# 128 bytes of padding ahead of the raw and split weights of a three-pass float32 matmul kernel

## The chip, the cores and the metric

The kernel runs on one core of one Trainium2 chip, as one launch. The metric is the device time of a run in microseconds (us); lower is better. The engines are TensorE (PE; its weight loads are listed apart as PEld), VectorE (DVE), ScalarE (ACT), GpSimd (POOL) and SyncE (SP, which issues most of the transfers). [...]

## The reference, cut to what matters

A batch of one sequence, 512 tokens of 1024 channels, goes through three layers in float32:

- layer 0: a short convolution with gates beside a multi-head latent attention (8 heads), then a squared-ReLU MLP of width 4096;
- layer 1: a conformer convolution module (GLU, depthwise convolution of 31 taps, layer norm, SiLU), then the same kind of MLP;
- layer 2: a forgetting attention (8 heads, with 16 meta tokens put in front) beside trailing-mean pooling, then a SwiGLU feed-forward of width 2816.

```
proj = h @ w_in                        # 1024 x 2208
ffn  = square(relu(h @ w1)) @ w2       # 1024 x 4096, 4096 x 1024
ffn2 = (silu(n2 @ w_gate) * (n2 @ w_up)) @ w_down
```

Nearly all the work is in such products of an activation of 512 tokens with a weight matrix that is read once.

## The kernel before

**Three passes a product.** Every float32 operand is split in two `float32r` parts, a high part and the rest (low). `mm3` issues three matmuls for each block of 128 x 128 weights: high weights by high activation (line 357), high weights by low activation (line 358), low weights by high activation (line 359). The weight block is the *stationary* operand, which a weight load (LDWEIGHTS) brings into the array; the activation, 128 partitions by 512 tokens, is the *moving* operand that streams past it. The weight load of the next matmul runs while the current matmul streams.

**Tiles.** Activations live in tiles named `P` ("token tiles"), `[128, 2, 512]` of 4 bytes, so 4096 bytes a partition: the high half first, the low half 2048 bytes on. Scratch tiles `S` are `[128, 544]` floats, 2176 bytes. The weights arrive from memory in `raw` tiles of 4096 bytes (line 271, on SP's queue, three in rotation) and are split into `W` tiles, `[128, 2, 512]` as well: ScalarE writes the high half (line 284), VectorE the low half (line 286; GpSimd in one stretch). A `W` tile holds four blocks of 128 columns, 512 bytes apart. Some matmuls read no `W` tile at all: attention scores (line 623: keys stationary, queries moving), their maxima (line 872) and the values times probabilities (lines 357 to 359 through `mm3`) have a `P` tile on both sides.

**Where the tiles lie.** The pools stand behind one another in each partition, in the order of their `with` lines: constants, `p` (32 tiles of 4096 bytes), `s` (9 tiles of 2176), then `r` (`raw`, 3 of 4096) and `w` (`W`, 9 of 4096). The pools of PSUM and DRAM take no room there. 4096 is 16 times 256, so all `P` tiles begin at one offset within 256 bytes; 9 times 2176 is 19584, which is 76 times 256 and 128 over. So `raw` and `W` tiles begin 128 bytes off the `P` tiles within 256, and every 128-column block in them too, since blocks lie 512 bytes apart and halves 2048.

**Order.** The orders of the two attention parts are written out by hand (`B1`, `B2`); the rest follows loops. The weights come in exactly the order in which they are used, split four blocks ahead of TensorE.

```
mm(ps, w[0], x[0], start=first, stop=False)
mm(ps, w[0], x[1], start=False, stop=False)
mm(ps, w[1], x[0], start=False, stop=last)
```

Of the kernel before, what the change touches and what calls it, by code (L numbers as in the profile page):

```python
# [11 lines left out]
F32 = mybir.dt.float32  # L12
# [7 lines left out]
DRAM = bass.MemoryType.DRAM  # L20
# [1698 lines left out]
def build(arrays, stop=None):  # L1719
    nc = bacc.Bacc("TRN2", target_bir_lowering=False, num_devices=1)  # L1720
    ap = {}
    for name, a in arrays.items():
        ap[name] = nc.dram_tensor(f"in_{name}", a.shape, mybir.dt.from_np(a.dtype), kind="ExternalInput").ap()
    ap["out"] = nc.dram_tensor("out_0", (D, T), F32, kind="ExternalOutput").ap()
    with tile.TileContext(nc) as tc:
        with tc.tile_pool(name="c", bufs=1) as cp, tc.tile_pool(name="p", bufs=NP) as pp, \
                tc.tile_pool(name="s", bufs=NS) as sp, tc.tile_pool(name="ps", bufs=8, space=PSUM) as psp, \
                tc.tile_pool(name="d", bufs=1, space=DRAM) as dp, \
                tc.tile_pool(name="r", bufs=3) as rp, tc.tile_pool(name="w", bufs=NW) as wp:
            Program(tc, ap, (cp, pp, sp, psp, dp, rp, wp), stop).run()  # L1730
    return nc

# [6 lines left out]
```

## Time and profile before

| what | value |
|---|---|
| time, median of 3 runs | 1793.89 us (1792.48 to 1795.05) |
| the profiled execution: its own time, its span | 1788.58 us, 1786.8 us |
| TensorE busy with matmuls | 1746.1 us, 98% of the span, 8828 matmuls |
| VectorE, ScalarE, GpSimd busy | 1092.6 us, 802.0 us, 272.4 us |
| mean granted TensorE clock | 0.996 |
| transfers | 167.26 MB, mean 94 GB/s |

The profile is one execution, taken apart from the timed runs. The ends of matmuls in it are modelled and overlap (a matmul of 512 columns is listed with some 395 ns while the next one starts some 232 ns after it), so a matmul's cost is read from the starts: the distance from one start to the next, or a stretch without idle time divided by the matmuls that start in it.

### The profile page before, as it was taken

How to read it: one execution, taken by the hardware profiler on the slowest of the kernel's cores; microseconds unless marked ns; L12 is line 12 of the kernel's file. 1: busy time of each engine (PE TensorE's matmuls, PEld its weight loads, DVE VectorE, ACT ScalarE, POOL GpSimd, SP SyncE). 2: the span in 40 equal slices, each digit the busy share in tenths (PEclk: the TensorE clock that was granted, in tenths of full speed). 3: DMA queues.
4: the chain of work that ended last, by engine and by line, in shares of the span. 5: the costliest groups of instructions: out<-in, count | busy, mean ns of one | idle time of the engine just before them, and what ended most of it. 6: DMA issues, size and time to landing. Idle time of an engine off the chain costs nothing.

```text
span 1786.8 us, 23140 instructions
## 1 busy us (share of the span) xinstructions
PE 1746.1 (98%) x8828; PEld 1455.2 (81%) x8828; DVE 1092.6 (61%) x1770; ACT 802.0 (45%) x1461; POOL 272.4 (15%) x339
## 2 busy tenths in 40 slices
PE   9999999999999999999999999989999999999999
PEld 7778888888888878998888888888787888888887
DVE  7988685344444789968544444488896554344442
ACT  6546655333333446576433333357675443232230
POOL 3413330000000365503000000042223200000000
PEclk9999999999999999999999999999999999999999
DMA  5232213222222133512222222222222222222221
GB/s 200 68 101 59 101 60 118 94 95 94 95 94 95 48 106 106 166 59 91 100 95 94 95 95 95 94 95 73 72 73 95 94 95 94 95 94 95 94 95 59
DMA packets 49887, 167.26 MB, mean 94 GB/s; under 512 B 6848, under 2 KB 7296, under 8 KB 49776
## 3 DMA queue, kind: packets, MB, share of 16 engines
q1 hardware_dynamic: 47776, 160.70, 27.0%
q0 software_dynamic: 1936, 5.07, 1.0%
q8 instruction: 69, 1.13, 0.3%
q14 instruction: 42, 0.34, 0.1%
q10 hardware_dynamic: 64, 0.02, 0.0%
HBM read 158.25 MB, written 4.19 MB: 91 GB/s over the span
## 4 chain that ended last, share of the span: by engine, by line
PE 81%; DVE 11%; issue 3%; ACT 2%; POOL 2%; DMA 1%; SPq 0%; POOLq 0%; DVEq 0%; ACTq 0%
PE ps L358 26%; PE ps L357 26%; PE ps L359 26%; DVE P L968 2%; DVE W L286 1%; PE ps L623 1%; DVE P L401 1%; DVE S L424 1%; POOL P L971 1%; ACT S L450 1%; DVE S L1477 1%; DVE P L398 1%; DVE S L422 1%; DMA P<-in_xT 1%; DVE P L636 0%
## 5 line engine op out<-in xcount | busy, mean ns | idle before, releaser
L357 PE MATMUL ps<-P,W 128*128 128x512 f32 (+1 forms) x2541 | 935.2, 368 | 6.9 <-DVE S L1130 3.1
L358 PE MATMUL ps<-P,W 128*128 128x512 f32 (+1 forms) x2541 | 932.1, 367 | 5.8 <-DVE P L401 5.8
L359 PE MATMUL ps<-P,W 128*128 128x512 f32 (+1 forms) x2541 | 930.9, 367 | 0.0
L284 ACT ACTIVATE W<-raw 128x512 fp32r<-128x512 f32 x578 | 356.9, 628 | 672.9 <-PE ps L359 586.3
L286 DVE TENSOR_TENSOR W<-raw,W 128x512 fp32r<-128x512 f32 x523 | 372.2, 719 | 396.8 <-ACT W L284 391.1
L357 PEld LDWEIGHTS ps<-P,W 128*128 128x128 f32 x2541 | 479.9, 189 | 93.2 <-DVE S L1130 3.5
L358 PEld LDWEIGHTS ps<-P,W 128*128 128x128 f32 x2541 | 480.3, 189 | 90.2 <-DVE P L401 7.2
L359 PEld LDWEIGHTS ps<-P,W 128*128 128x128 f32 x2541 | 480.0, 189 | 84.4 <-DVE W L286 0.4
L971 POOL TENSOR_TENSOR P<-P 128x256 f32<-128x256 f32 x48 | 45.5, 957 | 787.9 <-DVE P L968 786.8
L398 DVE TENSOR_TENSOR P<-S,P 128x512 fp32r<-128x512 f32 (+3 forms) x134 | 93.8, 705 | 50.5 <-ACT P L397 49.9
L397 ACT ACTIVATE P<-S 128x512 fp32r<-128x512 f32 (+3 forms) x134 | 81.4, 613 | 63.2 <-DVE S L1664 25.8
L286 POOL TENSOR_TENSOR W<-raw,W 128x512 fp32r<-128x512 f32 x55 | 73.6, 1369 | 38.0 <-ACT W L284 33.9
L1082 DVE SCALAR_TENSOR_TENSOR ps<-P,vec,ps 128x512 f32<-128x512 f32 x116 | 77.8, 745 | 0.0
L1029 DVE SCALAR_TENSOR_TENSOR S<-ps,S 128x512 f32<-128x512 f32 x64 | 43.7, 690 | 37.0 <-PE ps L359 36.7
L400 ACT ACTIVATE P<-P,vec 128x256 fp32r<-128x256 f32 (+1 forms) x80 | 43.7, 550 | 49.8 <-POOL P L971 30.3
L470 POOL TENSOR_TENSOR S<-S 128x256 f32<-128x256 f32 (+1 forms) x45 | 47.6, 1058 | 76.0 <-ACT S L469 73.6
L401 DVE SCALAR_TENSOR_TENSOR P<-P,vec 128x256 fp32r<-128x256 f32 (+1 forms) x80 | 53.2, 678 | 9.7 <-ACT P L400 9.5
L469 ACT ACTIVATE S<-P 128x256 f32<-128x256 f32 (+1 forms) x105 | 46.4, 473 | 17.8 <-DVE P L1056 11.8
L636 POOL TENSOR_TENSOR P<-S,P 128x512 fp32r<-128x512 f32 (+1 forms) x24 | 34.3, 1428 | 113.0 <-DVE P L635 96.1
L1049 DVE TENSOR_TENSOR P<-ps,P 128x512 f32<-128x512 f32 x42 | 29.1, 692 | 30.9 <-PE ps L359 30.9
L623 PE MATMUL ps<-P 128*128 128x512 f32 (+3 forms) x160 | 41.3, 376 | 1.8 <-DVE S L1443 0.8
L470 DVE TENSOR_TENSOR S<-S 128x256 f32<-128x256 f32 (+1 forms) x60 | 33.0, 550 | 14.5 <-ACT S L469 13.5
(262 smaller groups left out, 1295.6 us busy)
## 6 DMA issues: line engine op xcount, KB each, us to landing
raw<-in_w SPq DMA_DIRECT2D x286, 512.0 KB
P<-in_xT SPq DMA_DIRECT2D x8, 256.0 KB
P<-in_xT POOLq DMA_DIRECT2D x8, 256.0 KB, 5.6
keep<-P SPq DMA_DIRECT2D x8, 256.0 KB
P<-P SPq DMA_DIRECT2D x16, 128.0 KB
P<-keep POOLq DMA_DIRECT2D x8, 256.0 KB, 4.6
out<-P SPq DMA_DIRECT2D x7, 256.0 KB
raw<-in_w SPq DMA_DIRECT2D x2, 256.0 KB
```

The source lines that it names most:

```text
L284: nc.scalar.activation(out=w[:, 0, :cols], in_=r, func=AF.Copy)
L286: eng.tensor_sub(out=w[:, 1, :cols], in0=r, in1=w[:, 0, :cols].bitcast(F32))
L357: mm(ps, w[0], x[0], start=first, stop=False)
L358: mm(ps, w[0], x[1], start=False, stop=False)
L359: mm(ps, w[1], x[0], start=False, stop=last)
L397: nc.scalar.activation(out=hi, in_=src, func=AF.Copy)
L398: nc.vector.tensor_sub(out=lo, in0=src, in1=hi.bitcast(F32))
L401: nc.vector.scalar_tensor_tensor(out=lo, in0=src, scalar=scale, in1=hi.bitcast(F32), op0=OP.mult, op1=OP.subtract)
L470: (eng or nc.vector).tensor_add(out=acc, in0=acc, in1=t)
L623: mm(o[:m], k, q[:, pl, c0:], start=n == 0 and m == 128, stop=n == len(keys) - 1 and mask is None)
L971: ins = eng.tensor_add(out=x[k][:, cols], in0=x[k][:, cols], in1=m[k][:, cols]).ins
L1082: V.scalar_tensor_tensor(out=dst if dst is not None and t == taps[-1] else acc, in0=u, scalar=w, in1=acc, op0=OP.mult, op1=OP.add)
```

## The change

A pool `pad` with one tile of 32 floats a partition (128 bytes) is opened between the `s` pool and the `r` pool, and VectorE sets its first column to zero. The tile is never read. All `raw` and `W` tiles begin 128 bytes later; `P`, `S` and the constants stay where they were.

```diff
                 tc.tile_pool(name="s", bufs=NS) as sp, tc.tile_pool(name="ps", bufs=8, space=PSUM) as psp, \
-                tc.tile_pool(name="d", bufs=1, space=DRAM) as dp, \
+                tc.tile_pool(name="d", bufs=1, space=DRAM) as dp, tc.tile_pool(name="pad", bufs=1) as pad, \
                 tc.tile_pool(name="r", bufs=3) as rp, tc.tile_pool(name="w", bufs=NW) as wp:
+
+            nc.vector.memset(pad.tile([128, 32], F32, name="pad")[:, 0:1], 0.0)
             Program(tc, ap, (cp, pp, sp, psp, dp, rp, wp), stop).run()
```

The order of instructions on every engine stays as it was, but for that memset. It is the first instruction of VectorE's program, ahead of the constants `eps`, `halfpi`, `ones` and `onesf` and of the first split of the input (L401). VectorE's first rows of the change:

```order
L1725 UNCONDITIONAL_BRANCH
L1731 MEMSET pad 128x1
L482 MEMSET eps 128x1
L484 MEMSET halfpi 128x1
L486 MEMSET ones 128x128
L488 MEMSET onesf 128x128
L401 SCALAR_TENSOR_TENSOR P<-P,vec 128x512
```

The five rows behind the new one have moved down by one place.

## Rows read from the trace of the kernel before

**Rows 1.** The page, part 4: the chain that ended last, by engine.
```profile
PE 81%; DVE 11%; issue 3%; ACT 2%; POOL 2%; DMA 1%; SPq 0%; POOLq 0%; DVEq 0%; ACTq 0%
```

**Rows 2.** Groups of TensorE by line and shape: count, busy us, mean ns, idle.
```profile
L357 PE MATMUL ps<-P,W 128*128 128x512 f32 x1879 | 743.4, 396 | 5.0 <-DVE S L1130 3.1 <-ACT P L400 1.0 <-ACT W L284 0.9
...
L357 PE MATMUL ps<-P,W 128*128 128x256 f32 x654 | 188.6, 289 | 1.9 <-ACT P L397 0.8 <-ACT P L400 0.6 <-DVE P L1689 0.5
```

**Rows 3.** Stretches: from:to, length, busy PE PEld DVE ACT POOL, PEclk, DMA, GB/s.
```profile
0.00:42.00 42.00, 38.60 (x155) 29.99 (x156) 29.36 (x41) 25.86 (x43) 16.34 (x37) 1.00 0.57 199
42.00:270.00 228.00, 220.74 (x1132) 184.26 (x1131) 191.52 (x306) 130.72 (x245) 73.00 (x94) 1.00 0.25 81
270.00:595.00 325.00, 325.00 (x1441) 265.37 (x1440) 144.31 (x215) 118.33 (x197) 0.00 (x0) 1.00 0.28 95
595.00:647.00 52.00, 45.61 (x311) 42.11 (x309) 42.05 (x66) 27.18 (x59) 33.71 (x39) 0.97 0.25 82
647.00:750.00 103.00, 102.63 (x628) 91.62 (x629) 102.97 (x158) 54.38 (x92) 58.62 (x60) 1.00 0.38 123
750.00:830.00 80.00, 74.84 (x528) 70.64 (x527) 55.11 (x114) 56.92 (x124) 12.81 (x15) 0.98 0.23 73
830.00:1170.00 340.00, 340.00 (x1552) 279.70 (x1552) 161.35 (x259) 128.97 (x222) 4.74 (x5) 1.00 0.28 95
1170.00:1365.00 195.00, 181.12 (x1269) 152.29 (x1268) 171.59 (x338) 126.46 (x271) 57.47 (x75) 0.99 0.25 77
1365.00:1787.00 422.00, 417.58 (x1822) 339.21 (x1821) 194.31 (x282) 133.22 (x213) 15.72 (x16) 1.00 0.28 94
```

**Rows 4.** TensorE in order of time (start, us, line), 1202 matmuls apart.
```profile
300.25 0.39 PE L359 MATMUL ps<-P,W 128*128 128x512 f32 x1
...
579.56 0.40 PE L358 MATMUL ps<-P,W 128*128 128x512 f32 x1
```

**Rows 5.** The same, layer 0's attention; the first two are 30 matmuls apart.
```profile
191.24 0.39 PE L357 MATMUL ps<-P 128*128 128x512 f32 x1
...
198.04 0.85 PE L623 MATMUL ps<-P 128*128 128x512 f32 x3
198.72 0.40 PE L357 MATMUL ps<-P,W 128*128 128x512 f32 x1
```

**Rows 6.** Two short stretches of TensorE: length, busy, granted clock, DMA share, GB/s.
```profile
118.70:119.90 1.20, 1.20 (x7) 1.00 0.00 0
158.70:159.80 1.10, 1.10 (x6) 1.00 0.98 398
```

**Rows 7.** TensorE in order of time there: five matmuls apart, then four.
```profile
118.72 0.40 PE L357 MATMUL ps<-P,W 128*128 128x512 f32 x1
...
119.88 0.40 PE L359 MATMUL ps<-P,W 128*128 128x512 f32 x1
...
158.68 0.39 PE L358 MATMUL ps<-P 128*128 128x512 f32 x1
...
159.59 0.40 PE L359 MATMUL ps<-P 128*128 128x512 f32 x1
```

**Rows 8.** The forget gate's matmuls (stationary 8 columns wide), three matmuls apart.
```profile
1214.06 0.40 PE L357 MATMUL ps<-P,W 128*8 128x512 f32 x1
...
1214.74 0.40 PE L357 MATMUL ps<-P,W 128*8 128x512 f32 x1
```

**Rows 9.** TensorE in the SwiGLU part, 31 matmuls apart.
```profile
1433.91 0.40 PE L358 MATMUL ps<-P,W 128*128 128x512 f32 x1
...
1441.15 0.39 PE L359 MATMUL ps<-P,W 128*128 128x512 f32 x1
```

**Rows 10.** TensorE in the conformer's taps, 45 matmuls of 256 columns apart.
```profile
743.79 0.28 PE L359 MATMUL ps<-P,W 128*128 128x256 f32 x1
...
749.16 0.28 PE L359 MATMUL ps<-P,W 128*128 128x256 f32 x1
```

**Rows 11.** The chain in order of time: the first link on VectorE.
```profile
11.95 0.76 DVE P L401
```

## The prediction

> **What bounds the kernel now.** I read the chain that ended last first: TensorE holds 81% of it, VectorE 11% [rows 1]. Then the stretches [rows 3], to see where TensorE has no gap at all: from 270 to 595 us it is busy for 325.00 of 325.00 us, from 830 to 1170 for 340.00 of 340.00, from 1365 to the end for 417.58 of 422.00, and once the input is there it runs on to 42 us. These are the MLPs, the SwiGLU part and the wide projections; VectorE, ScalarE and the transfers have room there (from 270 to 595 us VectorE 144 us, transfers 0.28). So in some two thirds of the span the time is simply the number of matmuls times the distance from one start to the next, and I looked at that distance.
>
> [...]
>
> - Weights stationary, token tile moving, 512 columns: 1202 distances from 300.25 to 579.56 us, 279.31 us, so 232.4 ns each [rows 4].
> - Token tiles on both sides (scores, values), also 512 columns, the same three-pass order: 30 distances from 191.24 to 198.04 us, 6.80 us, so 226.7 ns each [rows 5]. The next distance with weights again is back at the longer distance.
>
> The matmuls are alike in shape, type and order. What differs is where the stationary block lies: a `P` block begins at the same offset within 256 bytes as the moving tile, a `W` block 128 bytes off. [...]
>
> Two other readings of these 5.7 ns can be weighed with rows. (a) Traffic: attention has fewer transfers around it. But from 118.70 to 119.90 us nothing is transferred (share 0.00), and weights still pace at (119.88 - 118.72)/5 = 232 ns; from 158.70 to 159.80 the transfers are at 0.98, 398 GB/s, and token pairs still pace at (159.59 - 158.68)/4 = 227.5 ns [rows 6, 7]. So it isn't traffic. (b) The place of `W` at the far end of the memory, rather than the offset. The forget gate speaks against it, weakly: its weights are 8 columns wide, so each row block k begins 32 bytes after the one before, and the block of k = 4 lies 128 bytes on, at the offset of the token tiles, though in a `W` tile. Its three matmuls take 0.68 us from 1214.06 to 1214.74 [rows 8], where three at 232.4 take 0.70. That is the resolution of the rows, for one block, with 8 columns only.
>
> Does anything smaller or larger than 256 bytes count? In the 30 short distances, the values of an odd head (the heads stand 64 columns of 4 bytes apart, so 256 bytes off) pace as the even ones do, all at 226.7 [rows 5]. After the change `W` lies a multiple of 256 off `P`, but not of 512 (the `P` and `S` pools together, 32 times 4096 + 9 times 2176 bytes, plus 128 make 150,784 = 294 times 512 + 256), so it is in the place of the odd heads.
>
> [...]
>
> **The change, part by part.** *The memset.* One more instruction at the head of VectorE, one column. The first VectorE link of the chain starts at 11.95 us, when the first token tile has come from memory [rows 11]; the memset lies in that wait. Uncovered, it would cost less than the 0.76 us that the split of 512 columns takes there. I take 0.
>
> *Engines off the path.* `raw` and `W` move together, so the splits keep the relative offset of source and result; nothing in their cost is expected to change, and VectorE has 180 us of room in the first long stretch [rows 3].
>
> *TensorE.* Each matmul between a token tile and weights of 512 columns goes from 232.4 to 226.7 ns if the offset is the cause: 5.7 ns. There are 1879 on each of three lines, 5637 in all [rows 2]. With 256 columns there are 3 times 654 = 1962; they pace at (749.16 - 743.79)/45 = 119.3 ns [rows 10], half of 226.7 is 113.3, so 6.0 ns each; no row shows a long run of 256 columns between token tiles, so this is bounded by 0 and 6.0, and I take the upper end since 512 columns are the nearest case and have the same 5.7 over their clean pace. All together 5637 x 5.7 + 1962 x 6.0 = 32.1 + 11.8 = 43.9 us: the ceiling. Not all of it reaches the end. By stretch [rows 3], some 5.7 ns for each matmul listed there:
>
> - 0 to 42, 270 to 595, 830 to 1170, 1365 to the end: 155 + 1441 + 1552 + 1822 = 4970 matmuls, TensorE without gaps but for 3 us at the start and 4 at the end. All of it counts: 28.3 us.
> - 42 to 270: 1132 matmuls, but about 230 of them already have token tiles on both sides, so some 900 x 5.7 = 5.1 us. TensorE is busy for 220.74 of 228 us and VectorE for 191.52, with short waits in both directions. I take half, 2.5 us (bounds 0 and 5.1).
> - 595 to 647, a boundary between layers: 311 x 5.7 = 1.8 us; TensorE waits for 6 of 52 us. Half: 0.9.
> - 647 to 750: 628 x 5.7 = 3.6 us, of which I take 0. VectorE is busy for 102.97 of 103.00 us with its half of the depthwise convolution; TensorE will just reach the layer norm earlier and wait for it. This is where the gain is given back.
> - 750 to 830: 528 x 5.7 = 3.0 us, TensorE busy for 74.84 of 80; half, 1.5.
> - 1170 to 1365: layer 2's attention with its many short matmuls and 14 us of waits; VectorE 171.59 of 195. Of 1269 matmuls few are of the two shapes; I put down 0.5.
>
> Sum 28.3 + 2.5 + 0.9 + 0 + 1.5 + 0.5 = 33.7 us. Where a stream starts anew the clean pace needs a few matmuls to settle (the distances just before 191 us are still uneven), so I take 33. The profiled execution would go from 1788.6 to 1755.6 us. It is 5.3 us under the median of the timed runs, 0.3%; on the median the same 33 us give 1760.9: **1761 us**. This case's own range goes from 26 us (the gapless stretches alone, without their 430 or so matmuls of 256 columns) to 44 (the ceiling): 1750 to 1768.
>
> **The rivals.** *Only part of it:* the pace depends on more than the offset (for instance on how the streams fall into step after each wait), so that a third to two thirds of the 33 us come: 1772 to 1783. For it: the clean pace needs several matmuls to settle after each interruption, and weights also stand beside moving tiles cut at other offsets. Against it: the clean pace holds without a break over 30 matmuls and four kinds of stationary blocks.
>
> *No effect:* the cause is the region in which `W` lies, or something else that goes with `W` tiles and not with their offset; the 232.4 ns stay. Then only the memset is new: 1794 us. [...] For it: every long series at 232 ns is of `W` tiles, every one at 227 of `P` tiles. Against it: rows 8, and that I find nothing else by which the two differ.
>
> *Slower:* streams of weights and tokens don't settle at the clean pace but at another repeating one. The trace has one: from 1433.91 to 1441.15 us, 31 distances of 233.5 ns [rows 9], 1.1 ns over the usual. If the new offset made this the pace everywhere, 4970 x 1.1 = 5.5 us come on top: 1799 us. It decides if the clean pace belongs to equal offsets within 512 bytes or more, not 256, for then `W` only moves from one wrong offset to another. The odd heads speak against it.
>
> **How the numbers follow.** The forecast 0.66; only part 0.14; no effect 0.13; slower 0.05; a gain beyond the ceiling 0.02. What a measurement of this kernel can tell from no change is about 0.2%, 3.6 us. Faster by more than that: 0.66 + 0.02 + nearly all of the part, 0.81; same 0.13; slower 0.06 with what is left. The range for 8 in 10 reaches from the ceiling, 1750, over the forecast's own 1768 and through the partial case to 1786; "no effect" and "slower" stay outside.
>
> **What would show it.** In the changed profile: the distance from start to start in the stretch of [rows 4] at 226 to 228 ns; taps of 256 columns at 113 to 115; the stretch from 270 to 595 us shorter by about 8 us (1441 x 5.7), the one from 830 to 1170 by 9, the last by 10; TensorE waiting longer for VectorE at the end of the convolution, by about 3 us. If the distance stays at 232.4, the offset is not the cause; if it falls and the time doesn't, a wait has taken its place, and the stretches will say where.

## The result and the profile after

| | before | after |
|---|---|---|
| time, median | 1794.07 us (1792.48 to 1795.05, 4 runs) | 1764.16 us (1760.81 to 1766.37, 4 runs) |
| the profiled execution: its time, its span | 1788.58, 1786.8 us | 1765.45, 1763.7 us |
| TensorE busy, mean granted clock (as a share of full speed) | 1746.1 us, 0.996 | 1723.2 us, 0.991 |

The ratio is 0.9833, with a 95% interval of 0.9814 to 0.9851: 29.9 us by the medians, where 33 were forecast (1761 us, range 1750 to 1786). The chain that ended last looks as it did [rows 1]:

```profile
PE 80%; DVE 11%; issue 3%; ACT 2%; POOL 2%; DMA 1%; SPq 0%; POOLq 0%; DVEq 0%; ACTq 0%
```

So TensorE is still the bound; what changed is its pace. In order of time, the profile after shows the same matmuls as [rows 5], [rows 4], [rows 10] and [rows 9], in this order (start, duration, line):

```profile
190.95 0.39 PE L357 MATMUL ps<-P 128*128 128x512 f32 x1
...
197.75 0.84 PE L623 MATMUL ps<-P 128*128 128x512 f32 x3
...
300.33 0.39 PE L359 MATMUL ps<-P,W 128*128 128x512 f32 x1
...
572.78 0.39 PE L358 MATMUL ps<-P,W 128*128 128x512 f32 x1
...
735.97 0.28 PE L359 MATMUL ps<-P,W 128*128 128x256 f32 x1
...
741.27 0.28 PE L359 MATMUL ps<-P,W 128*128 128x256 f32 x1
...
1419.26 0.39 PE L358 MATMUL ps<-P,W 128*128 128x512 f32 x1
...
1426.29 0.39 PE L359 MATMUL ps<-P,W 128*128 128x512 f32 x1
```

- Token tiles on both sides: 6.80 us for 30 distances, 226.7 ns, as before [rows 5].
- Weights by token tiles, 512 columns: 272.45 us for 1202 distances, 226.7 ns where [rows 4] had 232.4. This is the pace of the token pairs.
- The stretch that paced at 233.5 [rows 9]: 7.03 us for 31 distances, 226.8 ns.
- Taps of 256 columns: 5.30 us for 45 distances, 117.8 ns, against 119.3 [rows 10] and a forecast of 113 to 115.

By form, the two rows of [rows 2] have become these (count, busy, mean ns, idle before):

```profile
L357 PE MATMUL ps<-P,W 128*128 128x512 f32 x1879 | 735.0, 391 | 4.0 <-DVE S L1130 2.8 <-ACT P L400 1.2
...
L357 PE MATMUL ps<-P,W 128*128 128x256 f32 x654 | 190.0, 291 | 1.9 <-ACT P L397 0.8 <-ACT P L400 0.6 <-DVE P L1689 0.5
```

The 512-column group is 8.4 us less busy, the 256-column group 1.4 us *more*; the idle time ahead of them is about the same, so no wait has taken the place of the pace there.

Two more series show the same in full length. The longest unbroken one, the tail of the SwiGLU part, is 1442 distances of 512 columns; and behind layer 0's attention, where projections handle half the tokens at a time, there are 91 distances of 256 columns. In the profile before:

```profile
231.47 0.27 PE L358 MATMUL ps<-P,W 128*128 128x256 f32 x1
...
242.26 0.28 PE L359 MATMUL ps<-P,W 128*128 128x256 f32 x1
...
1441.84 0.39 PE L357 MATMUL ps<-P,W 128*128 128x512 f32 x1
...
1776.94 0.39 PE L359 MATMUL ps<-P,W 128*128 128x512 f32 x1
```

and the same matmuls after:

```profile
230.74 0.28 PE L358 MATMUL ps<-P,W 128*128 128x256 f32 x1
...
241.64 0.28 PE L359 MATMUL ps<-P,W 128*128 128x256 f32 x1
...
1426.97 0.39 PE L357 MATMUL ps<-P,W 128*128 128x512 f32 x1
...
1753.82 0.39 PE L359 MATMUL ps<-P,W 128*128 128x512 f32 x1
```

335.10 us became 326.85 (232.4 to 226.7 ns), but the half products went from 10.79 to 10.90 us (118.6 to 119.8 ns). Below these two are called **the long series** and **the half series**; they are the same matmuls in every kernel.

**Where the 23.1 us between the two profiles lie.** The program has four long unbroken series of 512 columns (1343, 1078, 310 and 1442 distances). Their ends split the program into pieces of the same matmuls in both traces:

| piece, us before | length before | length after | gained |
|---|---|---|---|
| start to 272.59 | 272.59 | 273.36 | -0.8 |
| 272.59 to 584.68, first series | 312.09 | 304.41 | 7.7 |
| 584.68 to 909.08, boundaries and convolution | 324.40 | 321.67 | 2.7 |
| 909.08 to 1159.58, second series | 250.50 | 244.37 | 6.1 |
| 1159.58 to 1368.82, layer 2's attention | 209.24 | 212.21 | -3.0 |
| 1368.82 to 1776.94, third and fourth series | 408.12 | 397.80 | 10.3 |

24.1 us come from the four series, 4173 distances at 5.8 ns each; all the rest of the program together lost 1.0. For two of the pieces without an unbroken series, and the end of the first piece, the view by stretches shows (length, PE, PEld, DVE, ACT, POOL busy, granted clock, DMA share, GB/s), before:

```profile
584.68:909.08 324.40, 312.47 (x1938) 280.90 (x1936) 248.46 (x419) 179.96 (x351) 109.88 (x118) 0.99 0.30 97
1159.58:1368.82 209.24, 195.36 (x1378) 166.24 (x1377) 178.92 (x351) 132.82 (x282) 61.29 (x81) 0.98 0.24 74
231.47:272.59 41.12, 37.23 (x281) 35.18 (x279) 38.79 (x68) 24.26 (x57) 16.80 (x19) 1.00 0.26 89
```

and after:

```profile
577.77:899.44 321.67, 310.39 (x1937) 281.85 (x1936) 247.07 (x419) 180.15 (x351) 109.33 (x118) 0.98 0.30 97
1143.81:1356.02 212.21, 197.88 (x1377) 169.21 (x1376) 179.39 (x351) 132.79 (x282) 62.55 (x83) 0.97 0.24 75
230.74:273.36 42.62, 38.86 (x281) 36.96 (x279) 38.83 (x68) 24.26 (x57) 16.82 (x19) 0.96 0.29 93
```

VectorE's busy time is the same within 1.4 us; what differs is the clock: 0.99, 0.98 and 1.00 before, 0.98, 0.97 and 0.96 after. In both traces it stands at 1.00 or 0.50 alone: ahead of the last matmul it is at 0.50 in four stretches of 3.4 us before (the first from 611.67 to 615.08 us), in seven of 3.4 us and one of 6.8 us after (the last from 1347.95 to 1354.77). Over the whole profile, the clock that was not granted is (1 - 0.991) x 1763.7 = 15.9 us after and (1 - 0.996) x 1786.8 = 7.1 before. These some 8 us (the clocks have three digits) are an estimate of the most that the clock can hide of the gain in this pair of profiles: it takes TensorE to be the bound wherever the clock was low. The four executions of the changed kernel show about half of that: 1760.81 us at 0.996, 1762.88 at 0.995, 1765.45 at 0.991 and 1766.37 at 0.990, so 4.6 us for 0.005. The lower clock is no property of the change: executions of the kernel before were granted 0.990 to 0.996, those of the changed one as well. At 0.996 the kernel before took 1788.58 to 1790.62 us in five executions, the changed kernel 1760.81 in one: 28 to 30 us, like the medians.

### The profile page after: what moved, and what is told of

Read it like the earlier page. It is cut to its first block, busy times and chain, and to the rows that moved or that the text cites. A ratio compares the mean times of both kernels' runs of the same rounds, so it can differ in the third digit from the quotient of the medians.

```text
span 1763.7 us, 23141 instructions
## 1 busy us (share of the span) xinstructions
PE 1723.2 (98%) x8828; PEld 1459.7 (83%) x8828; DVE 1091.3 (62%) x1771; ACT 802.3 (45%) x1461; POOL 272.2 (15%) x339
## 4 chain that ended last, share of the span: by engine, by line
PE 80%; DVE 11%; issue 3%; ACT 2%; POOL 2%; DMA 1%; SPq 0%; POOLq 0%; DVEq 0%; ACTq 0%
PE ps L358 26%; PE ps L357 26%; PE ps L359 26%; DVE P L968 1%; DVE W L286 1%; PE ps L623 1%; DVE P L401 1%; POOL P L971 1%; DVE S L1477 1%; DVE S L424 1%; DVE P L398 1%; DMA raw<-in_w 1%; ACT S L450 1%; DVE S L422 1%; DVE S L420 0%
## 5 line engine op out<-in xcount | busy, mean ns | idle before, releaser
L286 POOL TENSOR_TENSOR W<-raw,W 128x512 fp32r<-128x512 f32 x55 | 73.0, 1352 | 37.7 <-ACT W L284 33.7
L401 DVE SCALAR_TENSOR_TENSOR P<-P,vec 128x256 fp32r<-128x256 f32 (+1 forms) x80 | 54.2, 691 | 9.7 <-ACT P L400 9.5
```

The lines of the kernel that those rows point to most:

```text
L286: eng.tensor_sub(out=w[:, 1, :cols], in0=r, in1=w[:, 0, :cols].bitcast(F32))
L401: nc.vector.scalar_tensor_tensor(out=lo, in0=src, scalar=scale, in1=hi.bitcast(F32), op0=OP.mult, op1=OP.subtract)
```

## The experiments

Three theories of the faster pace. **A, the offset:** what counts is the distance, within 256 bytes, from the token tile that streams to the weight block that is loaded. **B, the place:** what counts is where `W` itself lies. **C, the raw tiles:** what counts is where the transfers land and the splits read. The first eight kernels are the kernel before with other padding; each pool below has one tile, of which one column is set and which is never read. Each of the eight ran once, with a profile; there the pace decides, the time (with that of the kernel before on the same chip) only confirms.

**Raw tiles moved, weights not.** 128 bytes ahead of `raw` and 128 more ahead of `W`, which then stands 256 off its old place, so at its old offset:

```diff
-                tc.tile_pool(name="d", bufs=1, space=DRAM) as dp, \
-                tc.tile_pool(name="r", bufs=3) as rp, tc.tile_pool(name="w", bufs=NW) as wp:
+                tc.tile_pool(name="d", bufs=1, space=DRAM) as dp, tc.tile_pool(name="padr", bufs=1) as padr, \
+                tc.tile_pool(name="r", bufs=3) as rp, tc.tile_pool(name="padw", bufs=1) as padw, tc.tile_pool(name="w", bufs=NW) as wp:
+            nc.vector.memset(padr.tile([128, 32], F32, name="padr")[:, 0:1], 0.0)
+            nc.vector.memset(padw.tile([128, 32], F32, name="padw")[:, 0:1], 0.0)
```

> 128 bytes of padding ahead of the raw tiles and 128 more ahead of the W tiles: raw stands at the token tiles' offset within 256 bytes, W doesn't (256 bytes further than before, so at its old offset). Theory A (weight block against moving tile): the distance between matmuls of 512 columns stays at 232.4 ns, the time at about 1794 us. Theory C (the raw tiles' transfers and the reads of the splits gain): 226.7 ns and about 1764 us.

Measured: 1793.75 us, the kernel before 1791.44. The long series in order of time:

```profile
1445.68 0.40 PE L357 MATMUL ps<-P,W 128*128 128x512 f32 x1
...
1782.15 0.40 PE L359 MATMUL ps<-P,W 128*128 128x512 f32 x1
```

336.47 us for 1442 distances, 233.3 ns: not the clean pace, but 0.9 ns over that of before (both paces occur at this offset; see the last section). Nothing is gained: C falls.

**Weights moved, raw tiles not.** Only the second of the two paddings.

```diff
-                tc.tile_pool(name="r", bufs=3) as rp, tc.tile_pool(name="w", bufs=NW) as wp:
+                tc.tile_pool(name="r", bufs=3) as rp, tc.tile_pool(name="padw", bufs=1) as padw, tc.tile_pool(name="w", bufs=NW) as wp:
+            nc.vector.memset(padw.tile([128, 32], F32, name="padw")[:, 0:1], 0.0)
```

> 128 bytes of padding between raw and W: only W stands at the token tiles' offset. Theory A: 226.7 ns at 512 columns and about 1764 us, as with the change. Theory C: 232.4 ns and 1794 us.

Measured: 1759.66 us. The long series:

```profile
1421.18 0.39 PE L357 MATMUL ps<-P,W 128*128 128x512 f32 x1
...
1748.03 0.39 PE L359 MATMUL ps<-P,W 128*128 128x512 f32 x1
```

326.85 us, 226.7 ns: the whole effect of the change, with the raw tiles where they were. A or B.

**All tiles moved.** The 128 bytes ahead of `P`, so that `W` has the very addresses of the changed kernel, but the token tiles are 128 bytes off it again:

```diff
-        with tc.tile_pool(name="c", bufs=1) as cp, tc.tile_pool(name="p", bufs=NP) as pp, \
+        with tc.tile_pool(name="c", bufs=1) as cp, tc.tile_pool(name="padp", bufs=1) as padp, tc.tile_pool(name="p", bufs=NP) as pp, \
...
+            nc.vector.memset(padp.tile([128, 32], F32, name="padp")[:, 0:1], 0.0)
```

> 128 bytes of padding ahead of the token tiles, so that token tiles, scratch, raw and W all move by 128 and W stands at exactly the address that the change gives it, but 128 off the token tiles as before. Theory A (what counts is the offset between the two): 232.4 ns and 1794 us. Theory B (what counts is where W itself lies, within 256 bytes or by its address): 226.7 ns and 1764 us.

Measured: 1795.55 us. The series of token pairs of [rows 5] (30 distances), and the long series:

```profile
196.11 0.39 PE L357 MATMUL ps<-P 128*128 128x512 f32 x1
...
202.91 0.39 PE L623 MATMUL ps<-P 128*128 128x512 f32 x1
...
1447.48 0.40 PE L357 MATMUL ps<-P,W 128*128 128x512 f32 x1
...
1783.95 0.40 PE L359 MATMUL ps<-P,W 128*128 128x512 f32 x1
```

Token pairs keep 226.7 ns though all of them have moved; weights at the good addresses pace at 233.3. B falls: it is the distance between the two operands, and neither's place.

**256 bytes of padding** (the change's diff with a tile of 64 floats; the raw tiles move along). The weights are then back at their old offset within 256, but at another within 512.

> 256 bytes of padding ahead of raw and W instead of 128. Theory A with a period of 256 bytes: as without padding, 232.4 ns and 1794 us. If the period is 512 (then the changed kernel's offset of 256 and this one's of 384 from the token tiles are different places, and nothing says that this one is bad): another pace; if any move of W away from its old place helps: 226.7 ns and 1764 us.

Measured: 1793.89 us. The long series:

```profile
1447.16 0.40 PE L357 MATMUL ps<-P,W 128*128 128x512 f32 x1
...
1782.26 0.40 PE L359 MATMUL ps<-P,W 128*128 128x512 f32 x1
```

335.10 us, 232.4 ns, exactly that of before. 128 off is as bad in one half of 512 bytes as in the other.

**A sweep of the padding**, with tiles of 8, 16, 24 and 48 floats in the change's diff: 32, 64, 96 and 192 bytes. Since the old offset is 128, the weights then stand 96, 64 and 32 bytes short of the token tiles within 256, and 64 past them. The four expectations, in this order:

> 32 bytes of padding: weights lie 96 bytes short of the token tiles' offset within 256 (160 past it). Theory A sharp (only equal offsets are clean): above 226.7 ns, some 232 at 512 columns, 1794 us. Theory A graded (the nearer the better): between the two, some 231 ns and 1786 us.

> 64 bytes of padding: weights lie 64 bytes short of the token tiles' offset. Sharp: some 232 ns at 512 columns, 1794 us. Graded: some 229.5 ns, 1779 us. If what counts is the offset within 64 bytes or 128, the first would be clean already before the change, so this run can only confirm that.

> 96 bytes of padding: weights lie 32 bytes short of the token tiles' offset. Sharp: some 232 ns, 1794 us. Graded: some 228 ns and 1771 us. If a window of 64 bytes is what counts: 226.7 ns and 1764 us. For matmuls of 256 columns, which the change left at 119.8 ns, any offset that brings them down to 113 to 117 ns would be worth up to 12 us more.

> 192 bytes of padding: weights lie 64 bytes past the token tiles' offset, the mirror image of 64 bytes of padding. Sharp: some 232 ns and 1794 us. Graded and symmetric: as with 64 bytes of padding. If the order in which two streams walk through the memory counts, the two sides differ, and one of the two is clean.

Measured (the kernel before on the same chip: 1795.47):

| weights minus token tile, within 256 | kernel | time, us | long series, us | ns each | half series, us | ns each |
|---|---|---|---|---|---|---|
| 0 | the change | 1764.16 | 1426.97 to 1753.82 | 226.7 | 230.74 to 241.64 | 119.8 |
| +64 | 192 bytes | 1792.06 | 1444.08 to 1780.55 | 233.3 | 231.90 to 242.23 | 113.5 |
| 128 | before | 1794.07 | 1441.84 to 1776.94 | 232.4 | 231.47 to 242.26 | 118.6 |
| -96 | 32 bytes | 1797.56 | 1449.44 to 1785.91 | 233.3 | 235.23 to 246.14 | 119.9 |
| -64 | 64 bytes | 1785.68 | 1444.14 to 1774.20 | 228.9 | 236.29 to 247.00 | 117.7 |
| -32 | 96 bytes | 1792.73 | 1444.71 to 1781.18 | 233.3 | 233.27 to 243.89 | 116.7 |

The row at -64 has two paces within one execution. Its first unbroken series (1343 distances) and its long series, in order of time:

```profile
277.37 0.40 PE L357 MATMUL ps<-P,W 128*128 128x512 f32 x1
...
590.73 0.40 PE L359 MATMUL ps<-P,W 128*128 128x512 f32 x1
...
1444.14 0.40 PE L357 MATMUL ps<-P,W 128*128 128x512 f32 x1
...
1774.20 0.39 PE L359 MATMUL ps<-P,W 128*128 128x512 f32 x1
```

313.36 us and 233.3 ns in the first, 330.06 us and 228.9 ns in the other. And with 192 bytes the half series and the long one disagree:

```profile
231.90 0.28 PE L358 MATMUL ps<-P,W 128*128 128x256 f32 x1
...
242.23 0.28 PE L359 MATMUL ps<-P,W 128*128 128x256 f32 x1
...
1444.08 0.40 PE L357 MATMUL ps<-P,W 128*128 128x512 f32 x1
...
1780.55 0.40 PE L359 MATMUL ps<-P,W 128*128 128x512 f32 x1
```

The half series is at its best here, 113.5 ns, about half of 226.7, where 512 columns are at their worst. It doesn't stand for all half products: the 86 distances just ahead of it, in the same profile, pace at 117.8 (10.13 us).

```profile
220.86 0.28 PE L357 MATMUL ps<-P,W 128*128 128x256 f32 x1
...
230.99 0.28 PE L359 MATMUL ps<-P,W 128*128 128x256 f32 x1
```

And at -32, the nearest to the clean offset that was tried, the long series is no better than at -96:

```profile
1444.71 0.39 PE L357 MATMUL ps<-P,W 128*128 128x512 f32 x1
...
1781.18 0.39 PE L359 MATMUL ps<-P,W 128*128 128x512 f32 x1
```

So the effect is not graded by distance: at 512 columns there are a few paces (226.7, 228.9, 232.4, 233.3), a series falls into one of them and keeps it for hundreds of matmuls, and the half series has another good offset than the long one. +32 and +96 were not tried.

**An offset for each width.** If 512 columns pace best at 0 and the half products at +64, both can be had: make each `W` tile 4352 bytes (17 x 256) and put the blocks that half products load 64 bytes further on in their tile. Nine such tiles take 2304 bytes more a partition than the nine of the change, so this first takes a control with eight, and with splits seven blocks ahead at the boundaries in place of eight. Three kernels, five rounds of timing on one chip: the change again, the control, the control with the shift. The diff is the shift against the change; in the control `half` returns False.

```diff
-NP, NS, NW = 32, 9, 9
+NP, NS, NW = 32, 9, 8
...
+    def half(self, b):
+        name, k, t = self.first[b]
+        return ((name == "wo" and t > 4) or (name in ("w10", "w11") and t < 4)
...
-            w = self.w_pool.tile([128, 2, T], F32R, name="W")
+            o = 16 if self.half(self.nsplit) else 0
+            w = self.w_pool.tile([128, 1088], F32R, name="W")[:, o:o + 1024].rearrange("p (a c) -> p a c", a=2)
...
-            self.W.more(8)
+            self.W.more(7)
```

> The changed kernel once more, timed beside the next two: about 1763 us; 226.7 ns at 512 columns, 119.8 at 256. What differs from its first profile is the number of short stretches at half clock, so this also tells how far these alone move the time (a kernel whose profile has a mean clock of 0.996 should be some 4 us shorter than one with 0.991).

> The control for the next kernel: the change, with 8 W tiles of 4352 bytes instead of 9 of 4096 (so that a block can be moved by 64 bytes inside its tile) and splits at most 7 blocks ahead in the boundaries instead of 8; no block is moved. Paces as with the change, 226.7 and 119.8 ns; the time the same within 2 us, or a few us more if the ninth tile was needed in the boundaries.

> The control, with the weight blocks of the half-width matmuls (256 columns, in the boundaries between layers and in the conformer's second projection; not the taps) moved by 64 bytes inside their tiles, so that they lie 64 bytes past the token tiles' offset, where 192 bytes of padding had 115.3 and 114.2 ns. If each width has its own good offset: 115 ns for these some 1500 matmuls and still 226.7 for the wide ones, 5 ns x 1500 = 7.5 us of TensorE's time, of which 3 to 6 us reach the end since VectorE and ScalarE set part of the boundaries: 1757 to 1760 us. If the good offset belongs to the kernel as a whole (all weights alike): 119 to 120 ns stay, and the time of the control.

Measured, with the kernel before at 1793.66 us (11 runs):

| kernel | time, us | ratio to before | profiled clock | long series, ns | half series, ns |
|---|---|---|---|---|---|
| the change again | 1764.07 (1762.72 to 1764.37, 4 runs) | 0.9835 (0.9817 to 0.9853) | 0.992 | 226.7 | 119.8 |
| control, eight larger tiles | 1782.48 (1777.49 to 1786.72, 6 runs) | 0.9938 (0.9920 to 0.9957) | 0.985 | 226.7 | 119.8 |
| the shift, eight larger tiles | 1778.41 (1773.42 to 1781.47, 6 runs) | 0.9916 (0.9896 to 0.9936) | 0.983 | 226.7 | 113.6 |

The result repeats. The shift does to the half series what the sweep promised, without touching the 512s; the 115 ns that were expected lie between the two paces shown above for 192 bytes, 113.5 and 117.8. But the ninth tile, with the eighth block ahead that it allows, is worth more than the shift: the control loses 18.4 us by the medians, with the paces unchanged, where a few us at most were expected, and so the time expected of the shift, 1757 to 1760 us, was missed too. The control's three stretches, of the same matmuls as those above:

```profile
583.59:912.60 329.01, 315.87 (x1938) 285.89 (x1936) 246.71 (x419) 181.60 (x351) 108.37 (x118) 0.97 0.27 95
1156.96:1371.31 214.35, 200.13 (x1378) 170.12 (x1377) 179.59 (x351) 132.76 (x282) 61.10 (x81) 0.95 0.23 73
233.09:279.18 46.09, 41.20 (x281) 38.37 (x279) 39.15 (x68) 24.79 (x57) 16.80 (x19) 0.93 0.23 81
```

They take 589.5 us together, against 576.5 in the profile after, 13 us more, at a lower clock in each. Only 2.9 us of it are idle time of TensorE (32.3 us against 29.4); 10.1 are longer busy time, at the lower clock. What brought the clock down is not shown: layer 2's attention, the second row, has a clock of 0.95 against 0.97 with no more idle time (14.2 us against 14.3). The shift's 4.1 us below the control are within the two intervals, which overlap.

**The same with nine tiles.** Room for the ninth is made by a smaller scratch area, which by the author's count moves everything by 8 times 256 bytes; the paces below agree with that. The diff is against the kernel with the shift.

```diff
-NP, NS, NW = 32, 9, 8
+NP, NS, NW = 32, 9, 9
-            self.W.more(7)
+            self.W.more(8)
-    nc = bacc.Bacc("TRN2", target_bir_lowering=False, num_devices=1)
+    nc = bacc.Bacc("TRN2", target_bir_lowering=False, num_devices=1, dynamic_dma_scratch_size=14336)
```

> Nine W tiles of 4352 bytes again (room is made by a smaller scratch area for indirect transfers, which moves everything by 2048 bytes, 8 times 256), splits eight blocks ahead as in the change, and the weight blocks of the 256-column half products 64 bytes further on in their tile. If each width has its own good offset and the eight tiles of the two runs before only cost waits at the boundaries, 512 columns pace at 226.7 to 226.9 ns, the halves at 114.5 to 115.5 in place of 119.8, and the time is 4 us under that of the change (its own 1764): 1757 to 1762. Rival: TensorE waits for VectorE and ScalarE where the halves stand, so that the faster pace turns into waits: paces as above, but 1763 to 1766, no different from the change. Other rival: the larger tiles cost something by themselves: 1767 or more, with the waits of the boundaries as long as with eight tiles.

Measured: 1762.46 us (1758.40 to 1763.02, 5 runs), the kernel before 1793.80 (9 runs), ratio 0.9829 (0.9813 to 0.9845). The paces are as expected: 226.7 ns in the long series, and 113.5 in the half series, which runs from 230.52 to 240.85 us. The stretches in the profile (this execution is the fastest of the five, clock 0.995):

```profile
575.73:895.09 319.36, 306.61 (x1937) 276.94 (x1936) 247.50 (x419) 179.87 (x351) 108.22 (x118) 0.99 0.29 98
1139.46:1349.02 209.56, 194.57 (x1378) 165.66 (x1377) 178.59 (x351) 132.80 (x282) 62.46 (x81) 0.98 0.23 74
230.52:271.31 40.79, 37.63 (x280) 35.63 (x279) 38.69 (x68) 24.25 (x57) 16.84 (x19) 0.96 0.25 87
```

569.7 us, 6.8 less than in the profile after; but that one was granted 0.991, and by the estimate above (1 - 0.991) x 1763.7 - (1 - 0.995) x 1756.7 = 7.1 us of clock lie between the two, enough to hold all of it. The larger tiles cost nothing by themselves, so the third case falls. Between the first two, 4 us or nothing, it stays open: the median is 1.6 to 1.7 us under that of the change, the intervals overlap nearly fully, and 1762.46 lies between the two ranges that were put down. No version is shown to beat the change.

## Why the prediction was right, point by point

- **The reading of the pace** (232.4 against 226.7 ns, and that the offset makes the difference) held to the last digit: 226.7 ns after, 5.7 ns a matmul, at a granted clock of 1.00 in both. It was an inference from two kinds of operands; the runs show it with the operands unchanged and only their distance moved. That 256 bytes is enough, which was argued from the odd heads, held in the 256-byte run (232.4 ns, as before).
- **The gapless stretches, 28.3 us**, were slightly too much. The four unbroken series gave 24.1. The term counted every matmul in those stretches, and those of 256 columns gave nothing (the half series went from 118.6 to 119.8 ns). The prediction put these at some 430; the trace has 85, 180 and 42 in the three long stretches, 307. Without them (4970 - 307) x 5.7 = 26.6.
- **The 256-column matmuls, 6.0 ns each, were mis-sized.** The two bounds were 0 and 6.0 and the upper end was taken, because 512 columns were the nearest case. Measured: taps 119.3 to 117.8 ns, the half series 118.6 to 119.8. The lower end was the better choice; on this term "the same offset" was even the wrong one, since the half series paces best at +64.
- **The partly hidden stretches** (2.5 + 0.9 + 0 + 1.5 + 0.5 = 5.4 us) can't be read off one pair of profiles. With what the gapless term holds beyond the series, the prediction has 33.7 - 4173 x 5.7 = 9.9 us for the three pieces outside the four series, and between the first two profiles these came to -1.0. Seven profiles, cut at the same matmuls, say more. At the old offset the three pieces take 806.2 us (before), 810.4 (raw tiles moved), 809.6 (all tiles moved) and 810.6 (256 bytes); at the new one 807.2 (after), 806.1 (the change again) and 801.5 (weights moved). The means lie 4.2 us apart, while single profiles of one offset lie up to 6 apart. So some of the 9.9 came, by these few profiles roughly 4. Two readings of [rows 3] made the terms wrong from the start: they price all matmuls alike, though 336 of the 1132 from 42 to 270 us, some 250 of the 311 and 434 of the 528 in the two boundaries have 256 columns, which gave nothing; and in layer 2's attention not few, but 457 of the 1269 have one of the two shapes, 204 of them 512 columns.
- **The convolution's own term, 0, was too low.** In the profile after, the matmuls of [rows 3] from 647 to 750 took only 0.5 us less, but at a clock of 0.98. At full clock, before and in the second profile of the change:

```profile
647.37:749.93 102.56, 102.56 (x628) 91.55 (x629) 102.53 (x157) 54.31 (x91) 58.25 (x60) 1.00 0.37 123
641.29:741.76 100.47, 100.47 (x627) 91.01 (x628) 100.45 (x153) 53.98 (x91) 58.17 (x60) 1.00 0.35 120
```

2.1 us came, of the 3.6 that the prediction worked out and did not count. The stretch has 240 matmuls of 512 columns and 384 taps, and 240 x 5.7 + 384 x 1.5 = 1.9 us is what their paces give. VectorE is busy throughout in both, but so is TensorE, and behind this stretch TensorE waits 1.7 us in both ahead of the layer norm's sums of squares; the 3 us of added waiting did not show. That the gain is given back here was wrong.

- **The total.** 33 us were put down and 29.9 measured; 24.1 from the series and roughly 4 from the rest agree with that. The terms missed in both directions (1.7 us too much for the matmuls of 256 columns in the gapless stretches, 2.1 too little in the convolution), so part of the closeness of the sum is luck. The step that went from the profiled time to the median mattered as much: taken from the first two profiles alone the gain is 23.1 us, since before's was a well-clocked execution (0.996) and after's was not (0.991). The step from 33.7 to 33, for matmuls that have yet to settle at the clean pace, is small beside this. The trace before shows such a start from 185.53 us, where token pairs follow weights: nine distances take 2.08 us, 231 ns each, the next thirteen 2.95 us, 226.9 each.
- **The rivals.** *Only part of it*, 1772 to 1783 us, is excluded by the time, and by the four series, which keep the clean pace throughout. *Slower* named a real thing: the pace of 233.5 ns [rows 9] is that of every long series at -96, -32 and +64 (233.3), and the kernels at these offsets take 1792 to 1798 us. It only belongs to other offsets than this one. *No effect* is excluded by the result, and place or raw tiles as the cause by the first three runs. Why TensorE paces by the offset is not shown: the same matmuls take 226.7 or 233.3 ns by the offset alone, and no run here takes the weight load or the moving stream away.

## What to carry to other kernels

Where TensorE has no gaps, read the distance from one start to the next by operand and by width, and compare it with the best pace that the same trace shows anywhere; 2.5% of it was 1.7% of the whole time here. The offset between stationary and moving tiles is set silently by the sizes of all pools that lie in between, so try paddings in small steps whenever a pool's size changes, and judge each width apart, for the best offset tried for the half series was among the worst for the long one. Compare profiles at like granted clock: between executions of the changed kernel, 0.005 of it went with 4.6 us.

## What had not been expected of the hardware

- The pace as a function of the offset is not smooth. At 512 columns 0 bytes gives 226.7 ns and its neighbour at -32 gives 233.3, as bad as any; -64 gives 228.9 in the long series and 233.3 in the first one of the same execution.
- The half series has its best pace, 113.5 ns, at +64, and 119.8 to 119.9 at 0 and at -96. Other half products at +64 pace at 117.8, in the same profile; what decides between the two was not tried.
- At 128 off a series can fall into either of two paces: the one of 310 distances from 1368.82 to 1441.15 us before is at 233.3, the next, from 1441.84, at 232.4. With 256 bytes of padding the 310 are at 232.4 (1374.42 to 1446.47 us) and the first series is at 233.3 (272.10 to 585.47). What decides it was not tried.
- With eight `W` tiles the mean clock was lower: 0.985 and 0.983 in the two profiles, 0.992 in that of the change beside them. In the stretches compared above TensorE's busy time grew by 10.1 us, its idle time by 2.9.
